# Four small edits to a one-core inference step: load order of natural rows, warming products, the due time of the first query tile, and the engine of a small copy

## The chip, the cores and the metric

The kernel runs on one core of one Trainium2 chip. The metric is the device time of one execution, in microseconds; a time is the median of several runs. The chip's engines are named as in the profile: TensorE (PE, its weight loads PEld), VectorE (DVE), ScalarE (ACT), GpSimd (POOL) and SyncE (SP), whose queue issues the DMAs.

## The reference

One layer of a streaming encoder, for a prompt of 2048 frames and a sample of 64 frames that continues a stream of 4096 cached frames, model width 1024, all in float32:

```python
h = rmsnorm(x, norm_g) @ w_in                       # columns: qa ka va za qb kb vb zb ga gb
qa, ka = rmsnorm of each 64-wide half head
oa = differential attention(qa, ka, va)             # 4 heads, two 64-d halves, chunk-causal, ALiBi
ob = retention(qb, kb, vb)                          # 4 heads, chunkwise recurrent
oa = rmsnorm(oa, subln_g) * 0.2 * silu(za)
ob = rmsnorm(ob) * silu(zb)
m  = sigmoid(ga) * (oa @ w_oa) + sigmoid(gb) * (ob @ w_ob)
y  = x + m @ w_out
```

The outputs are y, the new keys and values and the final retention states, for prompt and sample.

## The kernel before

**Precision.** Every large product is made from operands split in a high and a low part (`hi`, `lo`; `wh`, `wl`; `ogh`, `ogl`), with three products per tile: high by high, high by low, low by high. The high part is a cast, mostly on ScalarE, the low part a subtraction on VectorE or POOL.

**Planner.** The program is written by generators (tasks) that a loop in the Python code runs in order of priority. It keeps model clocks for each engine (`self.pe`, `self.act`, `self.dve`, `self.pool`, `self.dma`): `P`, `A`, `V`, `G` add the modelled cost of an instruction on TensorE, ScalarE, VectorE, POOL and return the time at which its result is due; `ld` and `st` issue a DMA on SP and return when it should have landed. A task that yields a time sleeps until `self.pe` has reached it. So the model times decide only the order in which instructions are emitted. The orders on TensorE, ScalarE and VectorE are kept as emitted; those of SP and POOL are arranged by the framework, which also sets the real waits. Buffers are counted by `take` and `give` (the tag's number in `BUFS`): two PSUM banks `mm`, two `s`, two `at`, one `pv`, one `tp`; three `ev` for what is on its way from a bank to memory.

**Stages.** (1) `opening` makes the products of the first four 128-row tiles with eight weight pieces while these arrive, in four banks at once (tags `s` and `at`), then tiles 4 to 8 one after the other in the `mm` banks (8 is the sample's 64 rows). `warm` issues products of a constant tile before. (2) The first half's other column groups follow. `strassen` makes the groups of 256 columns. (3) In the second half of the prompt (`transposed`) column groups are interleaved with attention: `qk_block` makes scores, `softmax`, `at_pv` transposes and multiplies with the values. (4) `out_stream` makes the merge: `og_fin` prepares the gated branch outputs (POOL product, ScalarE sigmoid, VectorE product, ScalarE cast `ogh`, VectorE subtraction `ogl`), `m_tile` multiplies them (lines 2427 to 2429), `m_fin` multiplies by the gates and adds both branches. The last stage multiplies by `w_out`.

**Names that the change touches.** `LOADS` (line 57) is the order in which `x_prep` loads the input: "T" and "U" are pieces of the transposed prompt, "N" a tile of 128 natural rows (tile 8 is the sample's 64), "I" the identity, "Y" the transposed sample. `x_stats` goes through the "N" entries in the same order and makes each row's root (square and sum on ScalarE, then logarithm and exponential there, four small instructions on VectorE, the last at line 497). The values' tiles are left unscaled by the roots until they are evacuated: the `fin` of `fin_va` (lines 1313 to 1365) and `fin_vb` wait until the tile's root is emitted and scale with it as they read the bank (lines 1336, 1338, 1340). A tile's `mm` bank is free after that.

`w_piece` (line 1020) casts a weight piece, `w_low` subtracts. `n` counts the pieces; 1 is the very first. `load_head` (line 1534) loads the keys and, for the first head only, the first two query tiles with `load_q`, which appends the tile and its due time to `self.qs`; `attn_head` (line 1606) sleeps until that time before it emits the tile's scores:

```python
q, tq = self.qs.pop(0)
yield tq
```

The merged tile has 256 prompt columns and 8 of the sample. `m_fin` copies the latter into `self.msf`; `sample_split` splits the collected tile when `self.msn` is reached.

## Time and profile before

| | us |
|---|---|
| median of three runs (1903.94 to 1907.93) | 1905.44 |
| the profiled execution | 1906.92 |
| its span, first to last instruction | 1905.1 |
| TensorE busy | 1879.9 |
| VectorE busy | 1284.8 |
| ScalarE busy | 962.1 |
| POOL busy | 606.4 |

The mean granted clock of TensorE is 0.995 of full rate. Times in the profile are counted from the span's start. A row of the timeline gives the start, the time, the engine, the line, the operation, and output and inputs by the program's names; in brackets stand the engine's idle time before it and what ended it.

### The profile page before, as it was taken

To read this page: it belongs to the slowest core of one execution; us is meant where nothing else is said; L and a number is where in the kernel's file an instruction comes from. 1 tells how busy PE (TensorE), PEld (TensorE's weight loads), DVE (VectorE), ACT (ScalarE), POOL (GpSimd) and SP (SyncE) were. 2 spreads that over 40 slices of the span, in tenths; PEclk is the share of its full clock that TensorE was granted. 3 is DMA by queue.
4 is the path that set the end of the run, shared out by engine and by line. 5 is a ranking of instruction groups with operands and counts; after the bars stand their busy time and mean duration, and the time that the engine had idled before them with its cause. 6 is when DMAs were issued, how large, how long until landed. Compare 5 with 4: busy or idle time off the path is not lost.

```text
span 1905.1 us, 32089 instructions
## 1 busy us (share of the span) xinstructions
PE 1879.9 (99%) x10916; PEld 1650.1 (87%) x10916; DVE 1284.8 (67%) x3058; ACT 962.1 (50%) x2169; POOL 606.4 (32%) x572
## 2 busy tenths in 40 slices
PE   9999999999998999999999999999999999999999
PEld 8777788888888888888888899999999999999887
DVE  4577857656565876786477575677685348887664
ACT  6535745445334665555455464555565545553221
POOL 2332555565651212221211212200211534432442
PEclk9999999999999999999999999999999999999999
DMA  8835665665647867364523643643512767886542
GB/s 276 278 112 164 184 189 166 193 195 165 199 137 201 235 187 195 117 200 125 168 72 93 170 139 105 163 112 89 148 52 72 232 189 225 249 251 214 172 155 78
DMA packets 362132, 317.47 MB, mean 167 GB/s; under 512 B 67312, under 2 KB 309616, under 8 KB 361968
## 3 DMA queue, kind: packets, MB, share of 16 engines
q1 hardware_dynamic: 361968, 315.42, 55.8%
q8 instruction: 86, 1.41, 0.3%
q14 instruction: 78, 0.64, 0.1%
HBM read 209.88 MB, written 104.60 MB: 165 GB/s over the span
## 4 chain that ended last, share of the span: by engine, by line
PE 91%; DMA 3%; DVE 3%; ACT 1%; issue 1%; SPq 1%; POOL 0%; DVEq 0%; ACTq 0%
PE mm L1075 34%; PE mm L925 8%; PE at L1749 3%; PE tp L925 3%; PE s L1637 2%; PE s L1638 2%; PE s L925 2%; PE pv L1729 2%; PE pv L1728 2%; PE pv L1727 2%; PE pv L925 1%; PE s L2552 1%; PE s L2553 1%; PE s L2551 1%; DMA ws<-in_w_in_dram 1%; DMA q<-qT 1%
## 5 line engine op out<-in xcount | busy, mean ns | idle before, releaser
L1039 POOL TENSOR_TENSOR wl<-ws,wh 128x512 fp32r<-128x512 f32 x125 | 169.6, 1366 | 340.6 <-ACT wh L1029 327.1
L1075 PE MATMUL mm<-xh,wh 128*128 128x256 f32 (+2 forms) x784 | 260.4, 332 | 0.0
L1075 PE MATMUL mm<-xl,wh 128*128 128x256 f32 (+2 forms) x784 | 254.9, 325 | 0.0
L1075 PE MATMUL mm<-xh,wl 128*128 128x256 f32 (+2 forms) x784 | 254.9, 325 | 0.0
L1075 PE MATMUL mm<-wh,xh 128*128 128x512 f32 x480 | 194.5, 405 | 2.9 <-DVE x_st L492 2.9
L1075 PE MATMUL mm<-wh,xl 128*128 128x512 f32 x480 | 189.1, 394 | 0.0
L1075 PE MATMUL mm<-wl,xh 128*128 128x512 f32 x480 | 188.6, 393 | 0.0
L1075 PEld LDWEIGHTS mm<-xh,wh 128*128 128x128 f32 x784 | 148.9, 190 | 10.6
L1075 PEld LDWEIGHTS mm<-xl,wh 128*128 128x128 f32 x784 | 149.0, 190 | 10.1
L1075 PEld LDWEIGHTS mm<-xh,wl 128*128 128x128 f32 x784 | 148.6, 190 | 9.9
L1677 ACT ACTIVATE row<-row,a_mx 128x1024 f32<-128x1024 f32 (+7 forms) x144 | 149.7, 1042 | 14.9 <-DVE a_mx L1656 14.9
L1765 DVE TENSOR_TENSOR atl<-at,ath 128x512 fp32r<-128x512 f32 (+1 forms) x144 | 93.3, 659 | 91.2 <-ACT ath L1763 90.8
L1510 POOL TENSOR_TENSOR r_y<-r_y,r_sq 128x256 f32<-128x256 f32 x32 | 29.5, 922 | 356.9 <-DVE r_sq L1507 263.6
L1763 ACT CAST ath<-at 128x512 fp32r<-128x512 f32 (+1 forms) x144 | 79.1, 564 | 108.2 <-PE at L1749 107.6
L1646 DVE CUSTOM_DVE_ANT_0 row<-s,dfar 128x512 f32<-128x512 f32 (+2 forms) x148 | 91.7, 632 | 56.8 <-PE s L1638 55.4
L1075 PEld LDWEIGHTS mm<-wh,xl 128*128 128x128 f32 x480 | 90.5, 189 | 20.7
L1075 PEld LDWEIGHTS mm<-wh,xh 128*128 128x128 f32 x480 | 90.6, 189 | 19.9 <-DVE x_st L492 3.4
L1075 PEld LDWEIGHTS mm<-wl,xh 128*128 128x128 f32 x480 | 90.8, 189 | 16.4
L1418 ACT COPY ev<-mm 128x256 f32<-128x256 f32 (+2 forms) x86 | 39.0, 453 | 120.6 <-PE mm L1075 73.0
L1699 DVE SCALAR_TENSOR_TENSOR row<-row,a_w 128x1024 f32<-128x1024 f32 (+5 forms) x88 | 98.8, 1129 | 0.0
L1637 PE MATMUL s<-K,q 128*128 128x512 f32 (+3 forms) x243 | 92.6, 383 | 4.7 <-DMA q<-qT 4.3
L1029 ACT CAST wh<-ws 128x512 fp32r<-128x512 f32 x128 | 77.7, 617 | 31.9 <-DMA ws<-in_w_in_dram 19.0
(526 smaller groups left out, 5534.3 us busy)
## 6 DMA issues: line engine op xcount, KB each, us to landing
ws<-in_w_in_dram SPq DMA_DIRECT2D x160, 256.0 KB, 3.4
q<-qT SPq DMA_DIRECT2D x128, 128.0 KB, 3.2
K<-kT SPq DMA_DIRECT2D x48, 256.0 KB, 4.4
V<-vN SPq DMA_DIRECT2D x24, 512.0 KB, 5.1
wz<-in_w_in_dram SPq DMA_DIRECT2D x32, 256.0 KB, 4.0
row<-in_cache_k_T_dram SPq DMA_DIRECT2D x32, 256.0 KB, 3.3
row<-in_cache_v_diff_dram SPq DMA_DIRECT2D x32, 256.0 KB, 3.2
mT<-mo SPq DMA_DIRECT2D x64, 128.0 KB, 3.3
```

What stands on the lines that cost most here:

```text
L925: nc.tensor.matmul(ps, w[:, c], xs[x][c], start=bool(tag) and c == 0 and i == 0, stop=c == 3 and i == 2, skip_group_check=True)
L1029: self.nc.scalar.copy(h, st)
L1039: self.nc.gpsimd.tensor_sub(l, st, h.bitcast(F32))
L1075: nc.tensor.matmul(ps, p, q, start=c == 0 and i == 0, stop=c == KC - 1 and i == 2)
L1418: nc.scalar.copy(ev, ps)
L1637: nc.tensor.matmul(ps, q1s, kk, start=True, stop=False)
L1646: nc.vector.tensor_tensor_reduce(out=row[:, k0:k0 + n], in0=ps, in1=tab, scale=-SLOPES[h], scalar=3.0e38, op0=ALU.add, op1=ALU.min, accum_ ...
L1677: nc.scalar.activation(u, u, AF.Exp, bias=mx, scale=-1.0, accum_out=lp[:, k:k + 1])
L1699: nc.vector.scalar_tensor_tensor(out=u0, in0=u1, scalar=w[:, 0:1], in1=u0, op0=ALU.mult, op1=ALU.add)
L1749: nc.tensor.transpose(at[:, w:w + 128], src, self.ident)
L1763: nc.scalar.copy(ah[:, :w], at[:, :w])
L1765: nc.vector.tensor_sub(al[:, :w], at[:, :w], ah[:, :w].bitcast(F32))
```

## The change

Four edits:

- In `LOADS` the "N" entries come in the order 4, 5, 6, 7, 8, 0, 1, 2, 3, where it was 4, 5, 0, 6, 1, 7, 2, 3, 8. The places of "N" among the other loads stay.
- The first weight piece's cast goes to VectorE; the warming products ahead of the opening's first product go from 10 to 4 (the 8 at the program's start stay).
- The due time of the first query tile is counted 4000 ns later. The load itself is issued where it was.
- The 128x8 copy of the sample's merged columns goes from VectorE to ScalarE, and the planner counts it there, after the sum it reads.

```diff
+FIRSTQ = 4000.0
...
-    [("U", c, 8) for c in range(4, 8)] + [(c, j, 8) for c, j in zip("NINNYNNNNN", (5, 0, 0, 6, 0, 1, 7, 2, 3, 8))]
+    [("U", c, 8) for c in range(4, 8)] + [(c, j, 8) for c, j in zip("NINNYNNNNN", (5, 0, 6, 7, 0, 8, 0, 1, 2, 3))]
...
-        self.nc.scalar.copy(h, st)
-        th = self.A(512, max(self.pe, t))
+        if n == 1:
+            self.nc.vector.tensor_copy(h, st)
+            th = self.V(512, max(self.pe, t))
+        else:
+            self.nc.scalar.copy(h, st)
+            th = self.A(512, max(self.pe, t))
         return self.w_low(wide, n, st, h, l, th, tag, tags)
...
             if c == 0:
-                self.warm(10)
+                self.warm(4)
...
             yield from self.load_q(0, 0)
+            q, t = self.qs[0]
+            self.qs[0] = q, t + FIRSTQ
             yield self.pe + 3000
...
         nc.vector.tensor_add(m, a, gs)
         t = self.V(GW, t)
-        nc.vector.tensor_copy(self.msf[:, ct, 8 * g:8 * g + 8], m[:, 256:GW])
-        self.msn = self.V(20)
+        nc.scalar.copy(self.msf[:, ct, 8 * g:8 * g + 8], m[:, 256:GW])
+        self.msn = self.A(8, t)
```

## The prediction, made before the changed kernel ran

> **What bounds the kernel now.** I read the page's totals first, then the waits of TensorE, then the granted clock in stretches around the longest waits, then the timeline at each place.

> ```profile
> span 1905.1 us, 32089 instructions
> ...
> PE 1879.9 (99%) x10916; PEld 1650.1 (87%) x10916; DVE 1284.8 (67%) x3058; ACT 962.1 (50%) x2169; POOL 606.4 (32%) x572
> ```

> TensorE bounds the span: only 1905.1 - 1879.9 = 25.2 us of it lie outside its products. An edit that leaves the products alone can win only from these gaps and from products run at a lower clock. The waits of TensorE say where the gaps are (line waited at, releaser, us in total, times, longest):

> ```profile
> PE s L1637 <- DMA q<-qT: 4.3, 1, 4.3
> PE at L2428 <- DVE ogl L2384: 3.3, 2, 2.6
> PE mm L1075 <- DVE x_st L492: 2.9, 1, 2.9
> ...
> PE tp L1277 <- DVE raw L1262: 1.6, 1, 1.6
> ...
> PE mm L1071 <- DVE x_st L492: 1.0, 1, 1.0
> ...
> PE s L1638 <- DMA q<-qT: 0.8, 2, 0.4
> ```

> The three longest are each touched by one part of the change. Each also costs more than itself. Stretches of TensorE (us, busy, instructions, granted clock, DMA share, GB/s):

> ```profile
> 58.00:66.00 8.00, 6.77 (x23) 0.79 0.96 333
> 598.00:608.00 10.00, 8.12 (x37) 0.66 1.13 301
> ...
> 1622.00:1632.00 10.00, 8.05 (x41) 0.66 0.97 292
> ...
> 120.00:140.00 20.00, 19.03 (x88) 1.00 0.64 203
> ```

> After each of the three the clock is granted at less than full: 8 x 0.21 = 1.7 us of work lost behind the wait of 2.9 us, 10 x 0.34 = 3.4 us behind the 4.3 us, 3.4 us behind the 2.6 us. The gap of about 1 us in the last stretch, and the 1.6 us wait among the waits, stand without such a row that I could find; between 1.6 and 2.6 us a wait begins to cost double. So the three places are worth 1.0 + 2.9 + 1.7 = 5.6, 4.3 + 0.4 + 3.4 = 8.1 and 3.3 + 3.4 = 6.7 us, 20.4 us in all. The question for each part is what is late next.

> **Part 1, the opening.** Six of 18 warming products go, and the first weight cast moves from ScalarE to VectorE.

> ```profile
> 0.00:5.00 5.00, 3.95 (x18) 1.00 0.51 145
> 0.00:7.10 7.10, 6.05 (x35) 1.00 0.60 184
> ```
> ```profile
> 7.74 0.62 ACT L1029 CAST wh<-ws 128x512 fp32r<-128x512 f32 x1 [1.05 <-DMA ws<-in_w_in_dram]
> ```
> ```profile
> 8.63 0.62 PE L1122 MATMUL at<-wh,xl 128*128 128x512 f32 x2
> 9.08 0.62 PE L1122 MATMUL s<-wh,xh 128*128 128x512 f32 x2
> ```

> Each warming product is two instructions. The first 18 take 0.22 us each, the next 17 0.12 us, so the 12 that go are of the cheap kind: 12 x 0.12 = 1.5 us. The first group of real products could start about 1 us sooner, but the second needs its weights cast, at 7.74 + 0.62 = 8.36 us behind a DMA, and begins at 9.08 now: at most 0.5 us is won, whatever the first cast costs on VectorE, which stood idle there. Were the array slower to reach full rate with fewer warming products, the 0.5 us would be lost instead. This must then cross the wait at 59 us, which hangs on something else (next). I take 0, bounds -0.5 and +0.5.

> **Part 2, the natural rows.** The order of the nine row tiles on SP's queue goes from 4 5 0 6 1 7 2 3 8 to 4 5 6 7 8 0 1 2 3; squares, roots and root chains follow in that order, the same work on ScalarE and VectorE. A full row tile now takes the last place, the half-size sample tile an early one. The wait it aims at, around tile 6's and 7's evacuation:

> ```profile
> 43.90 0.21 DVE L497 TENSOR_SCALAR xroot<-x_st 128x1 f32<-128x1 f32 x1
> ...
> 45.63 0.75 SPq L273 DMA_DIRECT2D row<-in_x_sample_dram  x1
> ...
> 48.08 0.62 ACT L1029 CAST wh<-ws 128x512 fp32r<-128x512 f32 x1 [4.29 <-DMA ws<-in_w_in_dram]
> ...
> 50.22 0.67 ACT L1336 ACTIVATE hi<-mm,xroot 128x512 fp32r<-128x512 f32 x1
> ...
> 54.49 0.62 ACT L1029 CAST wh<-ws 128x512 fp32r<-128x512 f32 x1 [0.87 <-DMA ws<-in_w_in_dram]
> ...
> 57.14 0.68 ACT L1336 ACTIVATE hi<-mm,xroot 128x512 fp32r<-128x512 f32 x1
> ...
> 59.23 0.50 PE L1075 MATMUL mm<-wh,xh 128*128 128x512 f32 x1 [2.93 <-DVE x_st L492]
> ```

> The sixth root written, tile 7's, is there at 43.90 + 0.21 = 44.1 us. Its tile is scaled only at 57.14 us, because ScalarE runs in order and stood 4.29 us at a weight cast whose DMA was late, 0.87 us at another. The roots of tiles 6 and 7 are not what is late; an earlier root alone moves nothing. What does change is the traffic: at 45.63 us SP issues 0.5 MB in place of 0.25 MB, ahead of the weights cast at 54.49 us; 0.25 MB at the 333 GB/s of the stretch at 58 us are 0.8 us. I take 0; the bounds are -5.6 us (both waits go, because ScalarE's order is dealt anew) and +0.8 us.

> **Part 3, the first query tile.** The planner is told that it lands 4 us later, so it puts about 4 us of other products ahead of the first score products. No load moves.

> ```profile
> 582.80:595.00 12.20, 12.17 (x102) 1.00 0.52 140
> ```
> ```profile
> 594.94 0.28 PE L1075 MATMUL mm<-xh,wl 128*128 128x256 f32 x1
> 599.52 0.45 PE L1637 MATMUL s<-K,q 128*128 128x128 f32 x1 [4.30 <-DMA q<-qT]
> ...
> 611.12 0.30 PE L1075 MATMUL mm<-xh,wh 128*128 128x256 f32 x1
> ```
> ```profile
> 599.34 0.54 SPq L278 DMA_DIRECT2D qbT<-ev  x1
> ```
> ```profile
> 603.56 0.37 ACT L1418 COPY ev<-mm 128x256 f32<-128x256 f32 x1 [11.48 <-DMA qbT<-ev]
> ...
> 610.61 0.37 ACT L1418 COPY ev<-mm 128x256 f32<-128x256 f32 x1 [4.93 <-DMA qbT<-ev]
> ```

> 102 products in 12.2 us are four groups of 24 and 6 of the fifth; 0.12 us each. The 18 left of the fifth fill 2.2 us, to about 597.2 us. The sixth group needs the bank of the fourth, and that is copied out at 603.56 us, because the copy waits 11.48 us for a store that SP issues at 599.34 us, behind the query loads. So TensorE would stand from 597.2 to 603.9 us, 6.7 us, where now it stands 4.3 + 0.4 us and then has scores to do. Behind that is a second wall: the seventh group starts at 611.12 us, right behind the copy at 610.61 us, which waits for another store. Work before 611 us that is only put in another order wins nothing unless the stores land sooner. I take 0; bounds -8.1 us (the stores do move up in SP's queue) and 6.7 - 4.7 = +2.0 us, more if the softmax, now queued on ScalarE behind the copy at 610.61 us, starves the next stage.

> **Part 4, the sample's merged columns.** 64 copies of 128x8 leave VectorE for ScalarE.

> ```profile
> 1620.00:1640.00 20.00, 17.37 (x118) 16.85 (x118) 18.52 (x38) 8.22 (x18) 10.28 (x9) 0.83 0.90 263
> ```
> ```profile
> L2454 DVE COPY msf<-mo 128x8 f32<-128x8 f32 x64 | 25.1, 392 | 2.2
> ```
> ```profile
> L2454 DVE COPY msf<-mo x64: 171/172/1197, 1555.8 to 1740.8; 128x8 f32<-128x8 f32 x64
> ```
> ```profile
> 1619.39 1.51 POOL L2367 TENSOR_TENSOR on<-on,z 128x528 f32<-128x528 f32 x1
> ```
> ```profile
> 1619.75 1.18 DVE L2454 COPY msf<-mo 128x8 f32<-128x8 f32 x1
> ...
> 1623.15 0.70 DVE L2384 TENSOR_TENSOR ogl<-on,ogh 128x528 fp32r<-128x528 f32 x1
> ```
> ```profile
> 30.93 0.20 ACT L488 ACTIVATE x_st<-x_st 128x1 f32<-128x1 f32 x1
> ```

> Here VectorE is the late engine (18.52 us of 20; ScalarE 8.22) and TensorE waits for its ogl. A copy costs 0.17 us alone, but 25.1 us in sum against 64 x 0.172 = 11.0: the rest is copies that stand beside a POOL instruction, like the one of 1.18 us that ends with POOL's at 1620.9. [...]

> Eight copies stand between 1605.9 and 1623.15 us. I count 0.1 us saved for each, and 0.2 us more for the long one, whose wait mostly passes to the next add: ogl comes about 1.0 us sooner, the wait of 2.6 us falls to 1.6, and the 0.7 us one (3.3 - 2.6) goes. 1.6 us is the size that showed no lower clock, so the 3.4 us go too: 1.0 + 0.7 + 3.4 = -5.1 us. On ScalarE a copy is 0.20 us (the nearest row), 64 x 0.20 = 13 us over 185 us in which it is half idle. The added wait: each copy stands behind its add on VectorE, and sigmoids and casts queue behind it. ScalarE now runs some us ahead of VectorE there; it will be held to VectorE's pace, and the casts that VectorE needs next come out just in time. Bounds: -6.7 us and, if ogl comes a wait of the same kind later, +6.0 us (2.6 + 3.4).

> [...]

> **Sum.** 0 + 0 + 0 - 5.1 us. The profiled execution took 1906.92 us (span 1905.1 and 1.8 around it), so 1901.8; the median of three, 1905.44, is 1.5 us below the profiled one, so I predict 1900.3 us for the median.

> All orders behind the first group are dealt anew, since the planner counts the first cast 0.1 us longer on VectorE (1.05 x 512 + 155 against 0.84 x 512 + 165 ns in the code) and 0.9 us is shifted in its DMA times. New waits of 1 to 2.6 us may appear anywhere, with 1.7 to 3.4 us of clock behind the longer ones; that is in the widths below.

> **The rivals.** First, the early waits go as well: SP's queue is dealt so that the stores land before TensorE needs their banks. For it: the waits hang on queue order, not on work. Against it: the loads and stores themselves are as many. With part 3 whole, 1900.3 - 8.1 = 1892.2; with part 2 too, 1886.6.

> Second, slower: the sixth group, put ahead of the scores, stands at its bank until 603.9 us. It decides if the store issued at 599.34 us still lands after 597.2 us; then +2.0 us, the first softmax starts at about 611 instead of 603.8 us, and one more gap with its lower clock (3.4 us) follows in the attention's first tiles, +5.4. If ScalarE's new waits also eat part 4's gain, that is 1905.4 + 5.4 = 1910.8.

> Third, the change does not do what it says: the rows' roots were not late, the query's gap only moves, VectorE's saved time is inherited by the adds. Then part 4 gives the 1.7 us without the clock, and the rest +-2: 1904, between 1901.7 and 1909.2.

> **How the numbers follow.** No change means within 0.2%, 3.8 us, about what a measurement of this kernel can tell. Forecast 0.33, early waits gone 0.15, slower 0.29, nothing 0.23. So faster 0.48, same 0.23, slower 0.29. The range from 1889 to 1911 leaves out the lower half of the first rival and the upper third of the second, some 0.17. Cases of both signs hold it; the forecast's own range is 1897 to 1903.

> **What would show it.** Part 1: the second group at about 8.6 us. Part 2: the wait at 59 us still there with roots 6 and 7 before 40 us; if it is gone with the late weight cast still there, I misread it. Part 3: the wait for q gone from the list and one for an ACT evacuation (a bank) in its place; the seventh group at 611 us as before. Part 4: no wait for ogl over 1.6 us and a clock of 1.00 from 1540 to 1745 us, L2452's mean above now. A total below 1893 would say that the stores moved; above 1909, that ScalarE or the bank took back more than VectorE gave.

## The result and the profile after

The changed kernel takes 1896.11 us (median of 6 runs, 1894.23 to 1899.38) against 1905.04 us before in the same comparison: a ratio of 0.9954, 95% interval 0.9942 to 0.9967, 8.9 us. Compared again later it gave 0.9938 (0.9925 to 0.9951). It is faster beyond what the measurement can confuse with no change.

In the changed kernel line numbers are 1 to 7 higher (492 is 493, 1075 is 1080, 1637 is 1644, 2384 is 2391, 1418 is 1423). The totals of its page:

```profile
span 1896.5 us, 32021 instructions
...
PE 1872.2 (99%) x10904; PEld 1643.2 (87%) x10904; DVE 1274.3 (67%) x2995; ACT 968.0 (51%) x2232; POOL 610.1 (32%) x572
```

TensorE's busy time fell by 7.7 us. The 12 cheap warming products that left it are some 1.5 us of that (12 x 0.12); most of the rest is products that ran at half clock before and run at full clock now. The time in which it stands fell little, from 25.2 to 24.3 us. Its waits (line waited at, releaser, us in total, times, longest):

```profile
PE mm L1080 <- ACT ev L1423: 6.8, 1, 6.8
PE mm L1080 <- DVE x_st L493: 2.1, 1, 2.1
PE tp L1282 <- DVE raw L1267: 1.6, 1, 1.6
PE s L1127 <- ACT wh L1034: 1.4, 1, 1.4
...
PE s L2435 <- DVE ogl L2391: 0.7, 1, 0.7
...
PE at L2435 <- DVE ogl L2391: 0.4, 1, 0.4
```

The wait for q is gone and a longer one, for ScalarE's copy out of a bank, stands at the same place; ogl's wait of 2.6 us at 1621 us is gone, and the longest one left in the merge is 0.7 us at 1681 us; the wait that begins at 56 us (and ended at 59 us before) shrank; a new one stands in the opening. Stretches of the changed kernel, then the four places of the kernel before at which the clock was halved, which means a granted clock of 0.50 (us, busy time of PE, PEld, DVE, ACT, POOL with instructions, granted clock, DMA share, GB/s):

```profile
58.00:66.00 8.00, 7.90 (x34) 6.49 (x35) 2.25 (x7) 4.79 (x9) 3.41 (x3) 1.00 0.97 337
600.19:607.01 6.82, 3.92 (x16) 3.92 (x16) 0.00 (x0) 0.37 (x1) 0.00 (x0) 0.50 1.15 319
720.00:745.00 25.00, 23.68 (x160) 21.67 (x160) 21.14 (x66) 14.75 (x40) 6.20 (x5) 1.00 0.86 232
1622.00:1632.00 10.00, 10.00 (x85) 10.00 (x84) 8.50 (x16) 6.72 (x17) 3.35 (x4) 1.00 0.81 248
```
```profile
60.03:63.44 3.41, 3.41 (x9) 2.64 (x8) 2.48 (x4) 2.16 (x4) 1.47 (x2) 0.50 1.00 330
599.33:606.16 6.83, 6.28 (x25) 6.12 (x26) 2.61 (x14) 2.13 (x9) 0.00 (x0) 0.50 1.11 312
732.45:735.86 3.41, 3.26 (x10) 3.10 (x11) 1.40 (x5) 0.00 (x0) 1.28 (x1) 0.50 1.10 259
1623.33:1630.16 6.83, 6.21 (x26) 5.90 (x27) 6.76 (x14) 3.88 (x9) 2.35 (x3) 0.50 1.00 297
```

Of four places one is left in this execution. Half of TensorE's busy time in such a place is counted as lost, an estimate from the clock of 0.50 (in the first place of before a 128x512 product starts every 0.43 us, right behind it every 0.23 us): 1.7, 3.1, 1.6 and 3.1 us before, 2.0 us now. With TensorE's waits over 0.25 us, read off the timeline, this gives an account by stage:

| stage, us | before: waits + clock | after: waits + clock | difference |
|---|---|---|---|
| opening, to the first product in an `mm` bank | ends 29.23 | ends 29.93 | +0.7 |
| the rest to 84 | 4.0 + 1.7 | 3.0 + 0 | -2.7 |
| 84 to 590 | 3.4 | 3.7 | +0.3 |
| 590 to 860 (first query tile) | 9.2 + 4.8 | 9.6 + 2.0 | -2.4 |
| 1550 to 1745 (merge) | 3.3 + 3.1 | 1.1 + 0 | -5.3 |

The sum is -9.4 us, the spans differ by 8.6. These are single executions; which of the small terms belong to the change is for the experiments.

### The profile page after: what moved, and what is told of

The parts are those of the page before. It is cut to its first block, busy times and chain, and to the rows that moved or that the text cites. A ratio compares the mean times of both kernels' runs of the same rounds, so it can differ in the third digit from the quotient of the medians.

```text
span 1896.5 us, 32021 instructions
## 1 busy us (share of the span) xinstructions
PE 1872.2 (99%) x10904; PEld 1643.2 (87%) x10904; DVE 1274.3 (67%) x2995; ACT 968.0 (51%) x2232; POOL 610.1 (32%) x572
## 4 chain that ended last, share of the span: by engine, by line
PE 89%; DMA 4%; DVE 3%; issue 1%; ACT 1%; SPq 1%; POOL 1%; DVEq 0%; POOLq 0%; ACTq 0%
PE mm L1080 33%; PE mm L926 8%; PE at L1756 3%; PE tp L926 3%; PE s L1644 3%; PE s L1645 3%; PE s L926 2%; PE pv L1736 2%; PE pv L1735 2%; PE pv L1734 2%; PE pv L926 1%; PE s L2560 1%; PE s L2559 1%; PE s L2558 1%; PE pv L2022 1%
## 5 line engine op out<-in xcount | busy, mean ns | idle before, releaser
L831 POOL TENSOR_TENSOR wl<-ws,wh 128x256 fp32r<-128x256 f32 x64 | 53.6, 838 | 121.6 <-ACT wh L822 105.4
```

Of the source, the lines that this page charges most:

```text
L831: nc.gpsimd.tensor_sub(l[:, cs], src, h[:, cs].bitcast(F32))
```

## The experiments

A comparison of the emitted programs comes first: TensorE's instructions stand in the same order in both kernels up to the first score products at 597 us and again from about 875 us on. Only part 3 changes that order, apart from the warming products. Parts 1 and 2 move a few instructions of the first 80 us on ScalarE, VectorE and SP; part 4 moves ScalarE's, VectorE's, POOL's and SP's order in the merge.

**Each part alone, on the kernel before.** The edits are the lines of the change itself.

Opening (4 warming products, first cast on VectorE):

> The kernel before with the opening's edit alone (4 warming products, first cast on VectorE). In the changed kernel the first product starts 0.96 us sooner (6.20 against 7.16 us), but the second group stands 1.37 us at its weights' cast, which waits for its DMA until 9.00 us (7.74 before), and the stage ends 0.70 us later. Theory A, the edit does this: second group at about 9.7 us, stage +0.7 us, and the wait of about 3 us at 59 us stays: total +0.5 to +1 us. Theory B, the weights' DMA landed late in that one execution by chance: second group at 8.6 to 9.1 us, total -0.5 to 0 us. Either way TensorE's order stays as before, so the waits at 595 and 1621 us are as before (4.3 and 2.6 us).

Natural rows in the new order:

> The kernel before with the new order of the natural rows alone. In the changed kernel the stage up to 84 us gave back 2.06 us: the wait of 1.0 us at 52 us is gone, the one at 56 us is 2.1 for 2.9 us, and the window at half clock (1.7 us lost) did not come; two new waits of 0.5 and 0.4 us came at 69 and 72 us. Theory A, the row order does it: total -1.5 to -2.5 us, no window at half clock near 60 us. Theory B, the later start of the opening did it (TensorE came 0.7 us later to the same bank, so it waited less): total 0 +-0.5 us here, the wait at 56 us again about 2.9 us and the window at half clock back.

First query tile counted 4 us later:

> The kernel before with the first query tile counted 4 us later alone. In the changed kernel the wait for q (4.3 us) turned into a wait of 6.8 us for an ScalarE copy out of a bank, the window at half clock behind it stayed 6.8 us long, and yet the stretch from 560 to 1000 us came out 2.7 us shorter: the waits of 2.4 us at 730 us and the 1.7 us of lower clock behind them are gone. Theory A, the edit re-deals TensorE's order from 597 to about 850 us and the stall at 730 us goes with it: bank wait 6.5 to 7 us, total -2 to -3.5 us. Theory B, the edit alone costs what the bank wait costs (+2 us) and the stall at 730 us was gone for another reason: total +1 to +3 us.

Copies on ScalarE:

> The kernel before with the 64 copies on ScalarE alone. Theory A, the copy on VectorE was what made ogl late: wait at 1621 us gone (under 1 us), no window at half clock from 1540 to 1745 us, total -4.5 to -6 us, and the waits at 56, 595 and 730 us as before. [...]

| alone | median, us (before 1907.69) | ratio | 95% interval |
|---|---|---|---|
| opening | 1904.46 | 0.9990 | 0.9978 to 1.0002 |
| rows | 1906.79 | 0.9998 | 0.9986 to 1.0010 |
| first query tile | 1905.13 | 0.9982 | 0.9972 to 0.9992 |
| copies | 1901.79 | 0.9970 | 0.9959 to 0.9982 |

Here and below the ratio is the comparison's own figure, not the quotient of the two medians (for the first query tile that would be 0.9987). A gain in us that stands beside a ratio is worked out from the ratio.

*Opening:* not theory A; the second group starts at 7.76 us here, earlier than either theory said, and the interval of the total holds 1. The two halves of this edit were not run apart. In the changed kernel's first trace its weights landed late in that execution:

```profile
9.67 0.74 PE L1127 MATMUL s<-wh,xh 128*128 128x512 f32 x2 [1.37 <-ACT wh L1034]
```

Over the 14 traces of this study the second group starts at 8.39 to 9.94 us with 10 warming products (seven traces, mean 9.1) and at 7.76 to 9.67 with 4 (seven, mean 8.5). With 10, the first product follows the last warming one without a gap in all of them, and it starts at 6.46 to 8.01 us; with 4 at 5.80 to 6.23. So the edit brings about 0.7 us at this place, and the landing of a DMA moves it by as much either way.

*Rows:* the wait at 56 us is 3.04 us and the half clock is there; alone the part does nothing that can be measured. *Query:* theory A, -3.4 us, with a bank wait of 7.1 us; the section on why the prediction was right shows where the gain is. *Copies:* theory A, -5.7 us, and no wait for ogl is left at all. All traces together say the same: in the merge (1550 to 1745 us) TensorE's waits and the loss at half clock come to 4.8 to 7.9 us in the five traces with copies and count as before, and to 0 to 1.1 us in the seven with the whole edit.

**Opening and rows together; query and copies together.**

> The kernel before with the row order and the opening's edit together, parts 3 and 4 left out. In the changed kernel they took 1.36 us off the stretch up to 84 us (+0.70 in the opening, -2.06 behind); alone, the rows gave a ratio of 0.9998 and the opening 0.999, each with an interval of about +-0.0012. Theory A, the two only shift which landing of a DMA is late, and the stage's end is set by the bank that waits on ScalarE in any case: total within 2 us of before, wait at 56 us between 2 and 4 us. Theory B, they work together: wait at 56 us about 2 us, no window at half clock near 60 us, total -2.5 us or more.

> The kernel before with the later query count and the copies on ScalarE, rows and opening as before. Alone they gave -3.4 us (0.9982) and -5.7 us (0.997). Theory A, these two are the whole gain and add up: -9 us, the same as the changed kernel (0.9954). Theory B, the opening and rows carry 1.5 to 2 us of the changed kernel's gain: -7 us here.

Opening and rows: 1906.03 us, 0.9993 (0.9985 to 1.0002). Query and copies: 1895.75 us, 0.9940 (0.9927 to 0.9953), both against 1907.27. Parts 3 and 4 give the gain, if anything more than the -9 us of theory A (-11.4). The changed kernel, which has all four parts, is not shown to be faster than this one (0.9954 and 0.9938 against 0.9940), so no total shows what parts 1 and 2 add. In the first run the total is theory A's, but the wait at 56 us is neither's: only 0.4 us of it is left, behind one of 2.0 us at 50 us and a half clock at 53 us. A row that all traces have tells more. The transposes behind the wait of 1.6 us near 140 us are the same instructions in every kernel, behind the same work of TensorE but for the warming products. In the timeline of before and of the changed kernel:

```profile
140.62 0.63 PE L1277 MATMUL tp<-ident,raw 128*128 128x128 f32 x4 [1.59 <-DVE raw L1262]
```
```profile
139.25 0.63 PE L1282 MATMUL tp<-ident,raw 128*128 128x128 f32 x4 [1.58 <-DVE raw L1267]
```

It starts at 139.97 to 141.76 us in six traces with neither part (mean 140.7), at 137.64 to 140.16 in six with both (mean 139.0), at 140.27 and 140.24 with one of them. So together they bring some 1.7 us up to there, beside which the ratio's 1.3 us fits, though its interval holds 1. Part of it shows in the chain of work that the profile follows back (start, time, what) and on ScalarE. The weight piece that ScalarE waits for, from its issue to its landing, before and changed, then ScalarE in the changed kernel:

```profile
46.49 7.98 DMA ws<-in_w_in_dram
```
```profile
46.33 7.00 DMA ws<-in_w_in_dram
```
```profile
53.35 0.62 ACT L1034 CAST wh<-ws 128x512 fp32r<-128x512 f32 x1 [0.63 <-DMA ws<-in_w_in_dram]
...
56.00 0.68 ACT L1341 ACTIVATE hi<-mm,xroot 128x512 fp32r<-128x512 f32 x1
```

The weights that ScalarE cast at 54.49 us before are cast at 53.35, and the bank behind them is read at 56.00 instead of 57.14. Their issue hardly moved (46.33 for 46.49 us); their landing came 7.0 us after it instead of 8.0. This time is 6.8 to 7.2 us in the six traces with both parts, 7.5 to 8.1 in the six with neither, 7.2 with the opening alone and 7.9 with the rows alone; the bank is read at 56.1 us in the mean of the first six and at 56.9 in the mean of the six with neither. So the opening, not the new row order, looks like what shortens it, but one trace of each part alone is thin, and why the landing is sooner is open.

**The copies: place or order?** The edit moves 64 copies and makes the planner deal the merge anew, that is, emit its instructions in another order. Two kernels separate this: the copy on ScalarE with the old count, and on VectorE with the new one.

```diff
-        nc.vector.tensor_copy(self.msf[:, ct, 8 * g:8 * g + 8], m[:, 256:GW])
+        nc.scalar.copy(self.msf[:, ct, 8 * g:8 * g + 8], m[:, 256:GW])
         self.msn = self.V(20)
```

> The kernel before with the 64 copies issued on ScalarE, but the planner still counts them on VectorE as before (20 columns, due as before), so that nothing else in TensorE's order and next to nothing in VectorE's and SP's order moves: only the place of the work changes. The full edit alone gave -5.7 us (0.997). Theory A, VectorE's time is what was short: here too -4.5 to -6.5 us, no wait for ogl over 1 us at 1621 us, no window at half clock there. Theory B, the gain came from the new deal of the merge's order that the other count brought: here 0 +-1.5 us, with a wait for ogl of 2 us or more at 1621 us.

```diff
         nc.vector.tensor_copy(self.msf[:, ct, 8 * g:8 * g + 8], m[:, 256:GW])
-        self.msn = self.V(20)
+        self.msn = self.A(8, t)
```

> The counterpart of the copies' change of place: the kernel before with the copies on VectorE as they were, but counted by the planner on ScalarE as in the change, so that the merge's order on ScalarE, VectorE, POOL and SP is the new one (TensorE's is the same in both). The place alone gave 0.9974, place and order together 0.997. Theory A, the place of the work is the cause: here 0.999 to 1.001, a wait for ogl of 1.5 us or more between 1590 and 1700 us. Theory B, the new order does as much by itself: 0.997 to 0.998 and no such wait.

Place alone: 1902.67 against 1907.27 us, 0.9974 (0.9962 to 0.9986). Order alone: 1904.74 against 1907.84, 0.9987 (0.9976 to 0.9998). Theory A held for the first, and neither for the second. The place is the larger share by these ratios, but the intervals overlap, and the one of the order alone ends just below 1. The waits of TensorE from 1550 to 1745 us, place alone, then order alone:

```profile
PE s L2428 <- DVE ogl L2384: 1.5, 1, 1.5
PE at L2428 <- DVE ogl L2384: 0.7, 1, 0.7
```
```profile
PE at L2428 <- DVE ogl L2384: 3.1, 4, 1.6
```

With the order alone TensorE waits 3.1 us, nearly as before (3.3), but no piece is over 1.6 us and the clock stays whole from 1550 to 1745 us. So in this trace the gain goes with a wait that was split and no half clock behind it. With the place alone the wait at 1621 us is gone; the longest one left is 1.5 us at 1683 us, and the clock is whole too. What became of VectorE's time is in the groups of the stretch 1550 to 1745 us, before and changed (line, engine, names, shapes, count, busy us, mean ns, idle before):

```profile
L2452 DVE TENSOR_TENSOR mo<-ga,gb 128x264 f32<-128x264 f32 x64 | 38.5, 601 | 0.9
...
L2373 DVE TENSOR_TENSOR on<-on,z 128x528 f32<-128x528 f32 x23 | 18.6, 814 | 2.9 <-DMA on<-oaT 2.5 <-DMA mT<-mo 0.3
```
```profile
L2459 DVE TENSOR_TENSOR mo<-ga,gb 128x264 f32<-128x264 f32 x64 | 46.2, 731 | 1.1
...
L2380 DVE TENSOR_TENSOR on<-on,z 128x528 f32<-128x528 f32 x23 | 21.1, 928 | 3.9 <-ACT z L2377 3.4 <-issue 0.2
```

Of the 25.1 us that the copies took, the same 64 adds take back 7.7 and the 23 products 2.5: what a copy took longer beside POOL, the next instructions take longer in part. Sorted by whether a POOL instruction overlaps them, the traces bear this out. Before, 38 copies stand beside none and take 0.17 us each, 26 stand beside one and take 0.71 us in the mean. The adds take 0.43 us in the mean beside none, before and after; beside POOL they take 0.81 us before (29 of them) and 0.98 after (35). Over the whole execution VectorE's busy time fell by 10.5 us (1284.8 to 1274.3). On ScalarE a copy takes 0.18 to 0.20 us, 12.4 us in all.

**The bank wait.** If it is the store's place on SP's queue, the second query tile's loads have to go behind the store.

```diff
             yield from self.load_q(0, 0)
             q, t = self.qs[0]
             self.qs[0] = q, t + FIRSTQ
-            yield self.pe + 3000
+            yield self.pe + 9000
             yield from self.load_q(0, 1)
```

> The changed kernel with the second query tile's loads held back (9000 for 3000 ns after the first's in the planner's count), so that the store of the first evacuated tile stands on SP's queue ahead of the second query tile's four loads instead of behind them. In the changed kernel those four issues took 3.4 us (594.67 to 598.07) and the store came at 598.17, its copy at 602.67, TensorE's wait was 6.8 us. Theory A, the wait is the store's place in the queue: store at about 594.7 us, bank wait 3 to 4 us, a shorter window at half clock, total 3 to 5 us below the changed kernel, if nothing downstream is late in its place (about -12 us against before). Theory B, the wait is the memory's load (the stretch shows a DMA share of 1.13), or a third thing is late at the same place: wait still over 6 us, total as the changed kernel (-8 to -9 us).

1895.00 us against 1907.27: 0.9934 (0.9923 to 0.9946). SP's queue of the changed kernel, then of this one:

```profile
594.67 3.40 SPq L274 DMA_DIRECT2D q<-qT  x4
598.17 0.54 SPq L279 DMA_DIRECT2D qbT<-ev  x1
```
```profile
593.28 0.38 SPq L279 DMA_DIRECT2D qbT<-ev  x1
...
596.07 2.53 SPq L274 DMA_DIRECT2D q<-qT  x4
```

And what the store lets go, ScalarE's copy and TensorE's group, in the changed kernel and in this one:

```profile
602.67 0.37 ACT L1423 COPY ev<-mm 128x256 f32<-128x256 f32 x1 [11.66 <-DMA qbT<-ev]
```
```profile
603.09 0.64 PE L1080 MATMUL mm<-xh,wh 128*128 128x320 f32 x1 [6.78 <-ACT ev L1423]
```
```profile
598.29 0.37 ACT L1423 COPY ev<-mm 128x256 f32<-128x256 f32 x1 [8.73 <-DMA qbT<-ev]
```
```profile
598.72 0.41 PE L1080 MATMUL mm<-xh,wh 128*128 128x320 f32 x1 [3.85 <-ACT ev L1423]
```

TensorE itself is 1.5 us ahead there. Beyond that the store is issued 3.4 us sooner, the copy starts 2.9 us sooner, the wait is 2.9 us shorter and the half clock behind it lasts 3.41 instead of 6.83 us. That is theory A for the wait. The shorter half clock is worth less than it looks: TensorE stood through part of the longer one, and lost 2.0 us there against 1.7 here. What is left is the store's landing (5.0 us from issue to copy here, behind 1.5 MB of key and query loads and a weight piece).

**Is the later due time still needed then?** The same with FIRSTQ at 0:

> The changed kernel with the second query tile's loads held back as in the run at 0.9934, and without the 4 us on the first tile's due time (FIRSTQ 0). Theory A, what makes TensorE stand near 596 us is the burst on SP's queue and in the memory, so once the store goes ahead of the second tile the 4 us are not needed: a wait of 2 to 4 us for q or for the bank, total within 2 us of 0.9934. Theory B, the due time matters by itself (its new order downstream took away the stall at 730 us): the wait for q 4 us again, a stall of 1.5 us or more between 700 and 860 us, 0.995 to 0.996.

1899.44 against 1907.84 us: 0.9959 (0.9946 to 0.9973), 4.8 us behind by the ratios. The bank wait is 3.8 us, as theory A has it, but the total is theory B's, with the loss in another place than it said:

```profile
PE pv L1734 <- ACT ath L1770: 5.8, 1, 5.8
PE mm L1080 <- ACT ev L1423: 3.8, 1, 3.8
```
```profile
641.04 0.58 ACT L1348 CAST hi<-mm 128x512 fp32r<-128x512 f32 x1 [7.98 <-DMA vN<-hi]
...
642.00 0.50 ACT L1770 CAST ath<-at 128x384 fp32r<-128x384 f32 x1
```

It is the same thing 40 us later: ScalarE stands 7.98 us at a cast whose buffer waits for a store, and the cast that TensorE needs is queued behind it. SP issues that store at 635.71 us, behind a burst of eight query loads (621 to 630 us) and the loads of rows after them.

**Repeats.**

> The changed kernel itself again, beside the others of this comparison, to set its parts against it. Its first comparison gave a ratio of 0.9954 (0.9942 to 0.9967), while its parts 3 and 4 alone gave 0.994 (0.9927 to 0.9953) and parts 1 and 2 0.9993. Theory A, the parts add up and the first comparison was at the upper end of its spread: 0.993 to 0.9945. Theory B, the parts work against each other: 0.9954 again. In the trace the bank wait at 596 us should again be 6.5 to 7.3 us and ogl's wait at 1620 us under 1 us in any case.

> The changed kernel with the second query tile's loads held back, again. It gave 0.9934 (0.9923 to 0.9946); the changed kernel itself gave 0.9954 and 0.9938 in two comparisons. Theory A, the bank wait of 3.9 in place of 6.8 us and the shorter window at half clock behind it (3.4 in place of 6.8 us) are worth 3 to 4.6 us each time: 0.992 to 0.9935 here. Theory B, what is saved there is taken back by waits that the new order brings later in the attention (1 to 1.5 us each in the first trace): 0.9935 to 0.995, no better than the changed kernel. In the trace the bank wait near 596 us should be 3.5 to 4.2 us either way.

The changed kernel again: 1895.79 against 1907.84 us, 0.9938; the bank wait is 6.6 us, ogl's longest 0.4. That is theory A, the parts add up, though the first comparison's 0.9954 was theory B's number. The version with the later second tile: 1893.93 against 1907.59 us, 0.9934 (0.9919 to 0.9949), bank wait 4.0 us, at the border between the theories. Twice 0.9934 against 0.9954 and 0.9938 are 0.8 to 3.8 us; the profiled spans, 1890.8 and 1891.6 against 1896.5 and 1895.7 us, are 4 to 6 us apart. It may be the best version here, but the intervals overlap, so that is not shown.

## Why the prediction was right, and where not

The forecast was -5.1 us, 1900.3, with a range of 1889 to 1911; measured were -8.9 us, 1896.1. The sign and the main mechanism (part 4) were right, the size was too small, and one term was taken wrongly. The range held the result, the forecast's own range of 1897 to 1903 just missed it, and with a chance of 0.48 for faster the sign was given little better than even odds.

**Part 4, -5.1 us: right.** Alone it gave -5.7 us, in the account -5.3. The lower clock went, as it said (3.1 us by TensorE's busy time, where the working had 3.4), and the mean of the adds rose, as it said (601 to 731 ns). But the working left 1.6 us of the wait at 1621 us, and in all eight traces with the copies on ScalarE that wait is gone: the 1.0 us that ogl was to come sooner was too little. That the clock at 1.6 us of wait would stay whole was therefore not put to the test there. These 1.0 us, with the part of the long copy's wait that was to pass to the next add, were an estimate, and no run shows the term; what the runs showed in its place is that VectorE's adds and products took back 10.2 us (7.7 + 2.5) of the copies' 25.1. Left out was the new order: it alone gave 0.9987. That ScalarE would be held to VectorE's pace and starve something did not show.

**Part 3, 0 us: the term that was wrong.** The working found three places with a lower clock. The trace of before has a fourth, and the wait that leads to it stands in the same list of waits:

```profile
PE tp L1637 <- DMA q<-qT: 1.7, 1, 1.7
```

It begins at 729.77 us, a second one for q (0.77 us) follows it, and the clock is halved from 732.45 us on. So here a half clock followed a wait of 1.65 us, with one of 0.77 us close behind, against the reading that a wait costs double only from between 1.6 and 2.6 us on. And this place lies where the edit gives TensorE a new order.

The mechanism of the second rival came as told: the wait for q became a wait for the bank of 6.78 us where the working had 6.7, released by a copy that waits for the store behind the query loads. But the account ended at 611 us, and the price of +2.0 to +5.4 us with it. TensorE's order is new up to about 875 us, and there the stall at 730 us (2.4 us of waits and 1.6 us of clock before) is gone. The other traces bear this out. From 700 to 860 us, TensorE's waits and the loss at half clock come to 2.9 to 5.0 us in the seven traces with the old order (mean 4.4; three of them have a half clock at 730 us), and to 0.7 to 1.3 us in the four with this edit and the loads as in the change (mean 1.0; longest wait 0.76 us, no half clock). From 590 to 700 us it is the other way: 8.4 us in the mean of the seven, 10.0 in the mean of the four. So the loss that the working priced at +2.0 us came, at +1.7, and the gain of 3.4 us behind it outweighed it. Alone the part gave -3.4 us by its ratio. A wait that moves from one place to another early in a stage was priced; the new order behind it was not. The run with FIRSTQ at 0 shows that such an order can as well cost 5.8 us, so the size of this term was not to be had from the trace of before. That 0 us is not further off is luck: a loss that the working had seen and a gain that it had not partly offset each other.

**Part 2, 0 us: right alone, perhaps too small with part 1.** "An earlier root alone moves nothing" held (0.9998), and the wait at 56 us stayed with roots 6 and 7 early. With the opening there is about 1.7 us at 140 us, which the working did not have; the weight piece issued at 46 us lands sooner then, for a reason that stays open. The 0.8 us counted against the larger load does not show (7.9 us from issue to landing with the rows alone, 7.5 to 8.1 with neither part). That the half clock near 60 us is gone from the changed kernel's first trace is not the edit's doing alone: four of the six traces with both parts have one between 53 and 61 us, as have all eight others.

**Part 1, 0 us with +-0.5: the bound was narrow.** The bound was read from one landing of a DMA (cast at 7.74 us), and even that row allows 0.7 us (9.08 - 8.36) where the working took 0.5. Over the 14 traces that cast starts at 6.6 to 9.0 us, a spread wider than the edit's 0.7 us.

**The sentence that all orders behind the first group are dealt anew was wrong.** Until 597 us TensorE's order is unchanged, and from about 875 us on again; for TensorE the width drawn from it belonged to part 3 alone. The first rival's total (1892.2) was near, but not by its mechanism: the stores did not move up. The experiment that moved one up came to 1895.0 and 1893.9 us, so that would have gone part of the way.

## What to carry to other kernels

When an edit turns a wait at a load into a wait at a buffer, follow the buffer to its store and the store to its place in the DMA queue: loads that nobody needs yet, issued ahead of a small store, held TensorE here for 2.9 us. Look for every place at which the clock is lowered before waits are sorted into cheap and dear. An account of a part that re-deals an order must run to where the orders meet again, not to the next wall. And a change in a merge that one engine paces is priced by what the engine's next instructions take back, at least 10 of 25 us here.
